# Delta-rule layer: one call inverts the triangles of several groups of a head, 27 calls in place of 48

## The chip, the core and the metric

The kernel runs on one core of a Trainium2 chip. The metric is device time in microseconds (us) of one launch, the median of several executions. The core has a matmul engine (TensorE, PE in the profile, with its weight loads as PEld), VectorE (DVE), ScalarE (ACT), GpSimd (POOL), and SyncE (SP), whose queue issues the DMAs. Each engine works through its own instructions strictly in the order in which the program was written.

## What is computed

Two layers of an encoder, for a prompt of 2048 tokens (16 tiles of 128) and one tile of 128 sample tokens: first a gated delta rule with 8 heads, then differential attention with 8 heads. The change is in the first layer. Per head and chunk the reference solves a unit lower triangular system and then carries a state from chunk to chunk:

```python
kb = k * beta[..., None]
A = jnp.where(strict, jnp.einsum("bnhid,bnhjd->bnhij", kb, k) * decay, 0.0)
sol = lax.linalg.triangular_solve(eye + A, rhs, left_side=True, lower=True, unit_diagonal=True)
...
def step(s, xs):
    u = u_i - jnp.einsum("bhcd,bhde->bhce", w_i, s)
    o = jnp.einsum("bhcd,bhde->bhce", qg_i, s) + jnp.einsum("bhij,bhje->bhie", qk_i, u)
    s = s * gl_i[..., None, None] + jnp.einsum("bhcd,bhce->bhde", kd_i, u)
    return s, o
```

The kernel takes chunks of 128 tokens, so that each tile of each head needs the inverse of one 128x128 unit triangular matrix.

## The kernel before

The tokens are taken in two halves: 9 tiles (tiles 0, 1, the sample tile, 2 to 7) and 8 tiles (8 to 15). Each half is cut into three groups: 3, 3, 3 tiles and 3, 3, 2 tiles. For each half `gdn_heads` runs the delta-rule layer, `out_proj` its output projection, then `diff_heads` and `out_proj` the attention layer. So the delta-rule stage comes twice.

No scheduler orders the work at run time. Generators (`projections`, `scans`, `others`, `inverse` and so on) write the program, and the class `Weave` (line 88) decides at build time whose next step is written, by its own estimates of when operands and buffers are ready and by a priority (`spawn`, line 221). The order so made is fixed; where its estimates are off, an engine waits.

What one head and group does in `gdn_heads` (line 955):

- `projections` (line 1023, priority 0): the projections to k, q and v, 72 matmuls of 128x384 per k, q or v in pieces of 3 (tiles `hT`, `wq`); then convolution and norms on ACT, DVE and POOL.
- `inverse` (line 1384): products of k with itself, times a decay matrix E, give X (a tile `X`, one 128x128 triangle per tile of tokens). X goes to a DRAM scratch area (`xd`), from which `blocks` (line 1335) fetches the 16x16 blocks of the diagonals, 8 per tile, one block per partition: 24 partitions for 3 tiles, 16 for 2 (tile `Lx`). DVE inverts them all at once, elementwise, in some 21 short instructions on `Lw`, `Lr`, `Lt`. The result goes through DRAM again (`wd`, tile `W`). From there PE doubles the blocks to 32, 64 and 128 by seven bursts of small matmuls, with copies on ACT or DVE between the bursts: `V,X` and `W,Y` (32x32, on four quadrants of the array), `V,X` and `W,Y` (32x32, on two), transposes of `Wf` (64x64), `F,X` (32x64) and `Wf,F` (64x64). The result is `Wf`.
- `scans` (line 1481): the state `S` goes from tile to tile. On PE this is `S,k`, then `y` on DVE, `y,Wf` on PE, `r` on ACT, `r,kd` on PE, and the new `S` on DVE, from which the next tile's `S,k` starts; `S,q` and `r,E` give the output.
- `others` (line 1007, priority -1): the gate projection of all tiles (`wz,hT`, and one quarter in `wq,hT`), which waits for nothing but its weights, and `first_outs` (line 823, priority -2), the first part of the output projection. These fill PE between the steps above.

`scans` waits for ("inv", h, gi) of one group before it takes the group's tiles. Buffers: `X` 3, `Wf` 3, `E` 4 or 5, `k` 5 or 6 (line 957), two each of `W16`, `W`, `V`, `Y`, `F`, two areas in DRAM, one `Lx` and `Lw`. 8 heads, 3 groups and 2 halves make 48 calls of `blocks`.

Of the kernel before, what the change touches and what calls it, by code (L numbers as in the profile page):

```python
# [12 lines left out]
F32 = mybir.dt.float32  # L13
# [3 lines left out]
ALU = mybir.AluOpType  # L17
# [4 lines left out]
P = 128  # L22
# [308 lines left out]
def body(ctx, tc, I, O):  # L331
# [100 lines left out]
    vs_d = [dram.tile([P, P], F32, name=f"vsd{h}") for h in range(H)]  # L432
    areas = [[dram.tile([3, n], F32, name=f"{k}{i}") for k, n in (("xd", P * P + P), ("wd", P * 16))] for i in range(2)]
    st_d = [dram.tile([P, P], F32, name=f"std{h}") for h in range(H)]
# [13 lines left out]
    def C(name):  # L448
        return loaded[name]
# [505 lines left out]
    def gdn_heads(hi_, tiles_of, pool, ahead):  # L955
        last = hi_ == len(HALVES) - 1
        NX, NWF, NE, NV, NK, NN, ND, NU = ((3, 3, 4, 2, 5, 3, 4, 3), (3, 3, 5, 2, 6, 6, 5, 4))[hi_]
        W.phase()
# [6 lines left out]
        def new(shape, tag, bufs, eng):  # L965
            return W.tile(pool, shape, F32, tag, bufs, eng)
# [368 lines left out]
        def blocks(area, nl):  # L1335

            X, Wl = (pool.tile([24, 16, 16], F32, name=k, bufs=1) for k in ("Lx", "Lw"))
            wf = Wl.rearrange("p i j -> p (i j)")
# [5 lines left out]
            yield "v"  # L1344
            T, R = (pool.tile([24, k], F32, name=nm, bufs=1) for k, nm in ((512, "Lt"), (64, "Lr")))

# [37 lines left out]
        def inverse(h, gi, d):  # L1384

            nt = len(tiles_of[gi])
            h0, h1 = slice(0, 64), slice(64, P)
            X = yield from new([P, 3, P], "X", NX, "v")
            yield ("E", h, gi),
            for i in range(nt):  # L1390
                yield from product(d, i, d["k"], X)
            W.done(("xq", h, gi))
            area = yield from W.hold(areas, "area", "sy")
            sy.dma_start(area[0][0:nt, 0:P * P].rearrange("t (p c) -> p t c", c=P), X[:, 0:nt])
            yield from blocks(area, 8 * nt)
            W16 = yield from new([P, 3, 16], "W16", 2, "sy")
            sy.dma_start(W16[:, 0:nt], area[1][0:nt].rearrange("t (p c) -> p t c", c=16))
            W.free(area)
            Wt = yield from new([P, 3, 32], "W", 2, "v")
            v.tensor_tensor(out=Wt[:, 0:nt].rearrange("p t (a c) -> p t a c", c=16),  # L1400
# [3 lines left out]
            W.free(W16)  # L1404
            V = yield from new([P, 3, 32], "V", 2, "v")
            Y = yield from new([P, 3, 32], "Y", 2, "s")
            F = yield from new([P, 3, 64], "F", 2, "s")
            pi = yield from bank("v")

            def area_of(o, n):  # L1410
                return pi[:, o:o + nt * n].rearrange("p (t c) -> p t c", c=n)

            pa, pb, pf, pt = area_of(0, 32), area_of(96, 32), area_of(192, 64), area_of(0, 64)
            quarters = [slice(32 * b, 32 * b + 32) for b in range(4)]

            def each(out, a, b):

                for o, x, y in zip(out, a, b):
                    pe.matmul(o, x, y, start=True, stop=True)

            def parts(t, rows, cols=slice(0, 32)):
                cols = cols if isinstance(cols, list) else [cols] * len(rows)
                return [t[r, i, c] for r, c in zip(rows, cols) for i in range(nt)]


            yield "v"
            v.transpose(V.rearrange("p t c -> p (t c)")[:, 0:32 * nt], Wt.rearrange("p t c -> p (t c)")[:, 0:32 * nt])
            yield "pe"
            each(parts(pa, quarters), parts(X, quarters, quarters), parts(V, quarters))
            yield "s"  # L1430
# [8 lines left out]
            yield "pe"  # L1439
            each(parts(pa, lower), parts(X, upper, lower), parts(V, upper))  # L1440
            Wf = d["Wf"] = yield from new([P, 3, P], "Wf", NWF, "g")
            e = W.either(nt * P)
            yield e
            getattr(W, e).tensor_tensor(
                out=Wf[:, 0:nt].rearrange("p t (a c) -> p t a c", c=32),
                in0=Wt[:, 0:nt, None, :].broadcast_to([P, nt, 4, 32]),
                in1=C("quart").rearrange("p (a c) -> p a c", c=32)[:, None].broadcast_to([P, nt, 4, 32]), op=ALU.mult)
            yield "s"
# [4 lines left out]
            yield "s"  # L1453
            for r, c in zip(upper, lower):
                s.copy(Wf[r, 0:nt, c], pb[r])

            for i in range(nt):
                yield "pe"
                pe.transpose(pf[h0, i], Wf[h0, i, h0], ident[0:64, 0:64])
            yield "s"  # L1460
            s.copy(F[h0, 0:nt], pf[h0])
            yield "pe"
            for c in range(64, P, 32):
                each(parts(pt, [slice(c, c + 32)], slice(0, 64)), parts(X, [h0], slice(c, c + 32)), parts(F, [h0], h0))
            W.free(X)
            yield "s"
            s.copy(F[h1, 0:nt], pt[h1])
            yield "pe"
            each(parts(pf, [h0], h0), parts(F, [h1], h0), parts(Wf, [h1], h1))
            yield "s"  # L1470
            s.copy(Wf[h0, 0:nt, h1], pf[h0])
            W.free(Wt, V, Y, F, pi)
            W.done(("inv", h, gi))

# [718 lines left out]
```

## Time and profile before

| what | value |
|---|---|
| median of 3 runs | 3585.93 us (3585.64 to 3587.45) |
| the profiled execution: its own time | 3588.79 us |
| its span (first to last instruction) | 3587.0 us |
| PE, DVE, ACT, POOL busy | 95%, 71%, 49%, 45% of the span |
| chain that ended last | PE 75%, DVE 11%, DMA 4%, POOL 4%, ACT 3% |
| first delta-rule stage | about 128 to 850 us of the span |
| second delta-rule stage | about 1870 to 2470 us |

A group's busy time is the union of its instructions. An idle time stands with the engine that ended it. One float32 matmul is two records of the trace; the listings of the program's order count it once, so 12 matmuls there are 24 in the trace.

### The profile page before, as it was taken

How to read it: one execution, taken by the hardware profiler on the slowest of the kernel's cores; microseconds unless marked ns; L12 is line 12 of the kernel's file. 1: busy time of each engine (PE TensorE's matmuls, PEld its weight loads, DVE VectorE, ACT ScalarE, POOL GpSimd, SP SyncE). 2: the span in 40 equal slices, each digit the busy share in tenths (PEclk: the TensorE clock that was granted, in tenths of full speed). 3: DMA queues.
4: the chain of work that ended last, by engine and by line, in shares of the span. 5: the costliest groups of instructions: out<-in, count | busy, mean ns of one | idle time of the engine just before them, and what ended most of it. 6: DMA issues, size and time to landing. Idle time of an engine off the chain costs nothing.

```text
span 3587.0 us, 79525 instructions
## 1 busy us (share of the span) xinstructions
PE 3420.1 (95%) x29336; PEld 3178.8 (89%) x29336; DVE 2556.4 (71%) x6345; ACT 1773.7 (49%) x5379; POOL 1622.3 (45%) x2758
## 2 busy tenths in 40 slices
PE   5999999999999999999999999998899999999988
PEld 2887789889999999998989899888899999999988
DVE  4677788775576666666467877775588888888872
ACT  3454455553354444444445555553365555555541
POOL 4344444443444434443344654444455455554442
PEclk6999999999999999999999999999999999999999
DMA  5225422235343333344531222225311112111113
GB/s 190 59 72 158 122 76 73 58 99 189 127 125 108 112 112 115 111 119 120 180 93 47 59 58 75 61 72 162 124 42 55 29 56 57 50 52 34 51 59 124
DMA packets 479420, 330.61 MB, mean 92 GB/s; under 512 B 65799, under 2 KB 442143, under 8 KB 479030
## 3 DMA queue, kind: packets, MB, share of 16 engines
q1 hardware_dynamic: 474358, 316.76, 30.0%
q0 software_dynamic: 4672, 8.78, 1.0%
q8 instruction: 230, 3.77, 0.4%
q14 instruction: 160, 1.31, 0.1%
HBM read 233.65 MB, written 91.77 MB: 91 GB/s over the span
## 4 chain that ended last, share of the span: by engine, by line
PE 75%; DVE 11%; DMA 4%; POOL 4%; ACT 3%; issue 3%; SPq 0%; POOLq 0%; DVEq 0%; ACTq 0%
PE ps L105 75%; DVE negm L105 1%; DVE Lt L105 1%; DVE p L105 1%; POOL p L105 1%; POOL fo L105 1%; DVE wq L105 1%; POOL sm L105 1%; DVE Lr L105 1%; ACT L105 1%; ACT jkg L105 1%; SPq L105 0%; DVE Lw L105 0%; DVE at L105 0%; DVE r L105 0%
## 5 line engine op out<-in xcount | busy, mean ns | idle before, releaser
L105 PE MATMUL ps<-wq,hT 128*128 128x256 f32 x6120 | 853.3, 287 | 4.4 <-DVE r L105 3.4
L105 PEld LDWEIGHTS ps<-wq,hT 128*128 128x128 f32 x6120 | 775.3, 190 | 17.5 <-DVE r L105 4.5
L105 PE MATMUL ps<-hT,wq 128*128 128x384 f32 (+1 forms) x3456 | 697.5, 341 | 2.1 <-ACT ub L105 1.6
L105 PE MATMUL ps<-wz,hT 128*128 128x256 f32 x4488 | 648.8, 291 | 14.2 <-DVE r L105 13.4
L105 PEld LDWEIGHTS ps<-wz,hT 128*128 128x128 f32 x4488 | 581.3, 193 | 23.8 <-DVE r L105 14.8
L105 PEld LDWEIGHTS ps<-hT,wq 128*128 128x128 f32 x3456 | 558.1, 190 | 15.3 <-issue 2.9
L105 ACT ACTIVATE p<-ps,negm 128x512 f32<-128x512 f32 (+3 forms) x640 | 396.9, 624 | 240.5 <-DVE negm L105 235.5
L105 DVE TENSOR_REDUCE negm<-ps 128x1 f32<-128x512 f32 (+3 forms) x640 | 377.7, 606 | 48.3 <-PE ps L105 37.9
L105 POOL TENSOR_SCALAR p<-p,fj 128x512 f32<-128x512 f32 (+2 forms) x320 | 247.1, 782 | 231.8 <-DVE fj L105 179.2
L105 PE MATMUL ps<-kst,qst 128*128 128x512 f32 (+3 forms) x1280 | 347.1, 380 | 0.4 <-ACT p L105 0.4
L105 PE MATMUL ps<-vpc,at 128*128 128x128 f32 x2176 | 294.4, 277 | 4.6 <-DVE at L105 4.0
L105 DVE SCALAR_TENSOR_TENSOR p<-p,fj,p 128x512 f32<-128x512 f32 (+2 forms) x320 | 274.2, 882 | 27.9 <-POOL p L105 27.0
L105 PEld LDWEIGHTS ps<-vpc,at 128*128 128x128 f32 x2176 | 271.4, 192 | 15.2 <-DVE at L105 8.8
L105 PEld LDWEIGHTS ps<-kst,qst 128*128 128x128 f32 x1280 | 206.6, 190 | 18.2 <-ACT p L105 2.7
L105 PE MATMUL ps<-cst_ident,p 128*128 128x128 f32 x1224 | 194.0, 275 | 16.1 <-DVE p L105 12.1
L105 POOL TENSOR_TENSOR wq<-st,wq 128x512 fp32r<-128x512 f32 x103 | 142.6, 1386 | 144.6 <-ACT wq L105 72.4
L105 ACT COPY at<-ps 128x512 f32<-128x512 f32 (+1 forms) x208 | 106.4, 512 | 188.5 <-PE ps L105 187.2
L105 ACT ACTIVATE jk<-ps 128x128 f32<-128x128 f32 (+1 forms) x212 | 80.3, 379 | 229.6 <-PE ps L105 177.2
L105 POOL TENSOR_TENSOR fo<-fo,cpow 128x1 f32<-128x1 f32 x280 | 173.9, 621 | 23.3
L105 PEld LDWEIGHTS ps<-cst_ident,p 128*128 128x128 f32 x1224 | 144.0, 141 | 25.3 <-DVE p L105 15.1
L105 POOL TENSOR_TENSOR r<-r,r 128x256 f32<-128x256 f32 (+1 forms) x144 | 106.2, 758 | 108.5 <-DVE r L105 106.7
L105 POOL TENSOR_SCALAR fo<-so,sm 128x1 f32<-128x1 f32 x136 | 51.0, 375 | 211.2 <-ACT jkg L105 210.9
(334 smaller groups left out, 6519.2 us busy)
## 6 DMA issues: line engine op xcount, KB each, us to landing
st<-in_w_in_gdn_dram SPq DMA_DIRECT2D x128, 256.0 KB
st<-in_w_in_diff_dram SPq DMA_DIRECT2D x256, 128.0 KB
x<-x SPq DMA_DIRECT2D x34, 512.0 KB
wz<-in_w_ada_dram SPq DMA_DIRECT2D x16, 1024.0 KB
sp<-in_cache_k_dram SPq DMA_DIRECT2D x64, 256.0 KB
sp<-in_cache_v_dram SPq DMA_DIRECT2D x64, 256.0 KB
zg<-zt SPq DMA_DIRECT2D x68, 128.0 KB
og<-o SPq DMA_DIRECT2D x136, 64.0 KB
```

Source lines behind the costliest of these rows:

```text
L105: r = f(*args, **kw)
```

## The change

`inverse` keeps the products that make X, one group at a time, and signals ("X", h, gi). A new generator `invert` takes a batch of groups, waits for all their X, and does the rest for all tiles of the batch together. `batches_of` sets the batches: in the first half the first group alone and the other two together (1 and 2 groups, 3 and 6 tiles), in the second half the whole head (8 tiles); the last head of each half stays group by group. That makes 7 x 2 + 3 calls in the first half and 7 + 3 in the second, 27 in all. `blocks` then works on up to 48 or 64 partitions. The scratch areas, `Lx`, `Lw`, `Lt`, `Lr` and the tiles of a call grow to 6 or 8 tiles; `W16`, `W` and `F` exist once instead of twice, V and Y become the two halves of F, and X has 4 buffers instead of 3. All matmuls stay: a burst of small matmuls has those of all tiles of its batch. `Wf` stays one tile per group, 3 in all, taken for the whole batch before its last bursts.

```diff
-        NX, NWF, NE, NV, NK, NN, ND, NU = ((3, 3, 4, 2, 5, 3, 4, 3), (3, 3, 5, 2, 6, 6, 5, 4))[hi_]
+        NX, NWF, NE, NV, NK, NN, ND, NU = ((4, 3, 4, 2, 5, 3, 4, 3), (4, 3, 5, 2, 6, 6, 5, 4))[hi_]
+        NTI = (6, 8)[hi_]
...
-            X, Wl = (pool.tile([24, 16, 16], F32, name=k, bufs=1) for k in ("Lx", "Lw"))
+            X, Wl = (pool.tile([8 * NTI, 16, 16], F32, name=k, bufs=1) for k in ("Lx", "Lw"))
...
         def inverse(h, gi, d):
 
-            nt = len(tiles_of[gi])
-            h0, h1 = slice(0, 64), slice(64, P)
-            X = yield from new([P, 3, P], "X", NX, "v")
+            batch = next(b for b in batches_of(h) if gi in b)
+            if gi == batch[0]:
+                W.spawn(invert(h, batch), 3)
+            X = d["X"] = yield from new([P, 3, P], "X", NX, "v")
             yield ("E", h, gi),
-            for i in range(nt):
+            for i in range(len(tiles_of[gi])):
                 yield from product(d, i, d["k"], X)
             W.done(("xq", h, gi))
+            W.done(("X", h, gi))
+
+        def batches_of(h):
+
+            if h == H - 1:
+                return [[gi] for gi in range(NGr)]
+            return [[0], list(range(1, NGr))] if hi_ == 0 else [list(range(NGr))]
+
+        def invert(h, batch):
...
+            at = [(gi, i) for gi in batch for i in range(len(tiles_of[gi]))]
+            nt = len(at)
+            yield ("X", h, batch[0]), "sy"
             area = yield from W.hold(areas, "area", "sy")
-            sy.dma_start(area[0][0:nt, 0:P * P].rearrange("t (p c) -> p t c", c=P), X[:, 0:nt])
+            for gi in batch:
+                yield ("X", h, gi), "sy"
+                sy.dma_start(...)
             yield from blocks(area, 8 * nt)
-            W16 = yield from new([P, 3, 16], "W16", 2, "sy")
+            W16 = yield from new([P, NTI, 16], "W16", 1, "sy")
...
-            Wt = yield from new([P, 3, 32], "W", 2, "v")
+            Wt = yield from new([P, NTI, 32], "W", 1, "v")
...
-            V = yield from new([P, 3, 32], "V", 2, "v")
-            Y = yield from new([P, 3, 32], "Y", 2, "s")
-            F = yield from new([P, 3, 64], "F", 2, "s")
+            F = yield from new([P, NTI, 64], "F", 1, "v")
...
-            Wf = d["Wf"] = yield from new([P, 3, P], "Wf", NWF, "g")
+            for gi in batch:
+                U[h, gi]["Wf"] = yield from new([P, 3, P], "Wf", NWF, "g")
...
-            W.done(("inv", h, gi))
+            for gi in batch:
+                W.done(("inv", h, gi))
```

The order moves everywhere in the two stages. Three places on PE matter below. First, one burst of small matmuls in the second stage: `V_30380,X_29967` before, where a group of two tiles has its own call:

```order
L105 MATMUL ps_81<-V_30380,X_29967 32x32 x8
L105 MATMUL ps_76<-hT_23573,wq 128x256 x6
L105 MATMUL ps_78<-r,kd_29567 128x128
L105 MATMUL ps_81<-W_30369,Y_30385 32x32 x8
L105 MATMUL ps_77<-k_29726 128x128
L105 MATMUL ps_76<-hT_23573,wq 128x256 x9
```

And in the changed kernel, where `F_30396` holds V and Y, and the three X are those of one head:

```order
L105 MATMUL ps_80<-F_30396,X_30070 32x32 x2
L105 MATMUL ps_82<-q_29909,k_29887 128x128
L105 MATMUL ps_80<-W_30386,F_30396 32x32 x32
L105 MATMUL ps_79<-cst_ident,k_30077 128x128 x3
L105 MATMUL ps_77<-cst_ident,q_30175 128x128 x3
L105 MATMUL ps_78<-wq,hT_22508 128x256 x9
```

The bursts of three groups have become one; counted over the whole program there are 337 bursts of small matmuls before and 189 after, and 1450 runs of the large projection matmuls before and 1392 after.

Second, the end of the second delta-rule stage on PE before. `wq,hT` is the gate projection, its last 21 matmuls stand first; `S,k`, `y,Wf` and `r,kd` are the state's steps; after 22 rows of such steps the output projection (`wz,hT_31711`) comes in:

```order
L105 MATMUL ps_77<-wq,hT_23573 128x256 x21
L105 MATMUL ps_80<-k_31317 128x128
...
L105 MATMUL ps_82<-y,Wf_31897 128x128
L105 MATMUL ps_81<-V_32168,X_31812 32x32 x12
L105 MATMUL ps_82<-r,kd_31089 128x128
...
L105 MATMUL ps_81<-V_32168,X_31812 32x32 x6
L105 MATMUL ps_75<-wz_30618,hT_31711 128x256 x3
L105 MATMUL ps_81<-W_32157,Y_32169 32x32 x6
```

The same place in the changed kernel, from its last gate projection to its first output projection:

```order
L105 MATMUL ps_81<-wq,hT_23259 128x256 x3
L105 MATMUL ps_80<-r,kd_29343 128x128
L105 MATMUL ps_78<-S,q_28953 128x128
L105 MATMUL ps_78<-r,E_29135 128x128
L105 MATMUL ps_77<-S,k_29129 128x128
L105 MATMUL ps_77<-y,Wf_30577 128x128
...
L105 MATMUL ps_81<-r,E_30342 128x128
L105 MATMUL ps_78<-S,k_30077 128x128
L105 MATMUL ps_76<-wz_29857,hT_30746 128x256 x9
```

There are 81 rows between them now, 32 of them `S,k`, `y,Wf` or `r,kd` (6 before), and no large matmul.

Third, a place in the middle of the second stage in the changed kernel, behind the last matmuls of one quarter of the gate projection (`wz_25955`); `hT_22508,wq` is the next projection to k:

```order
L105 MATMUL ps_82<-wz_25955,hT_23259 128x256 x3
L105 MATMUL ps_78<-r,kd_26293 128x128
...
L105 MATMUL ps_78<-S,k_26160 128x128
L105 MATMUL ps_78<-y,Wf_27655 128x128
L105 MATMUL ps_75<-hT_22508,wq 128x384 x6
```

17 rows with 9 steps of the state stand there without a large matmul. Two more such places have 7 steps (first stage, near its last head) and 5 steps (second stage). Before, the only other place with more than three steps has 4.

## Rows read from the trace of the kernel before

**Rows 1.** Busy time by stretches: stretch, its length, PE, PEld, DVE, ACT, POOL, granted clock, DMA.
```profile
128.00:850.00 722.00, 697.07 (x6335) 622.15 (x6334) 552.53 (x1538) 368.05 (x1205) 321.65 (x704) 0.98 0.35 96
1870.00:2470.00 600.00, 570.49 (x5422) 524.07 (x5421) 463.04 (x1258) 327.98 (x1083) 295.27 (x597) 0.97 0.25 68
```

**Rows 2.** What PE waited for, 1860 to 2500 us: total us, times, longest.
```profile
PE ps L105 <- DVE S L105: 9.4, 4, 5.3
PE ps L105 <- DVE y L105: 6.4, 7, 2.8
PE ps L105 <- DVE V L105: 4.8, 3, 4.1
```

**Rows 3.** Instructions that touch tile Lx: count, durations, first and last start, forms.
```profile
L105 DVE COPY Lw<-Lx x48: 155/167/726, 138.1 to 2422.6; 24x12 f32<-24x12 f32 x40, 16x12 f32<-16x12 f32 x8
```

**Rows 4.** Timeline of DVE: start us, us, instruction; first of one block inversion, and its follower.
```profile
2409.24 0.17 DVE L105 COPY Lw<-Lx 24x12 f32<-24x12 f32 x1
...
2415.26 0.33 DVE L105 SCALAR_TENSOR_TENSOR S<-S,g_eGl,ps 128x128 f32<-128x128 f32 x1
```

**Rows 5.** Timeline of PE: each burst of small matmuls with the row behind it.
```profile
159.83 0.64 PE L105 MATMUL ps<-V,X 32*32 32x32 f32 x24 [0.51 <-DVE V L105]
160.40 0.49 PE L105 MATMUL ps<-q,k 128*128 128x128 f32 x2
...
2397.62 0.46 PE L105 MATMUL ps<-V,X 32*32 32x32 f32 x12
2398.01 0.49 PE L105 MATMUL ps<-k 128*128 128x128 f32 x2
...
2404.12 0.66 PE L105 MATMUL ps<-F,X 64*32 64x64 f32 x12
2404.71 0.49 PE L105 MATMUL ps<-q,k 128*128 128x128 f32 x2
...
2441.18 0.35 PE L105 MATMUL ps<-V,X 32*32 32x32 f32 x16
2441.45 0.63 PE L105 MATMUL ps<-wz,hT 128*128 128x256 f32 x3
...
2450.39 0.42 PE L105 MATMUL ps<-F,X 64*32 64x64 f32 x8
2450.74 0.44 PE L105 MATMUL ps<-cst_ident,k 128*128 128x128 f32 x2
```

**Rows 6.** Timeline of PE: a short and a long run of large matmuls, with the rows behind.
```profile
2394.72 0.62 PE L105 MATMUL ps<-wq,hT 128*128 128x256 f32 x3
2395.18 0.38 PE L105 MATMUL ps<-k 128*128 128x128 f32 x2
...
2410.61 2.72 PE L105 MATMUL ps<-wq,hT 128*128 128x256 f32 x21
2413.17 0.38 PE L105 MATMUL ps<-k 128*128 128x128 f32 x2
2413.39 0.39 PE L105 MATMUL ps<-S,q 128*128 128x128 f32 x2
```

**Rows 7.** Timeline of PE at the end of the second stage, idle time before in brackets.
```profile
2415.74 0.46 PE L105 MATMUL ps<-S,k 128*128 128x128 f32 x2 [1.74 <-DVE S L105]
...
2418.74 0.42 PE L105 MATMUL ps<-S,k 128*128 128x128 f32 x2
...
2432.72 0.79 PE L105 MATMUL ps<-S,q 128*128 128x128 f32 x2 [5.35 <-DVE S L105]
...
2434.46 1.01 PE L105 MATMUL ps<-wz,hT 128*128 128x256 f32 x3
```

**Rows 8.** Busy time by stretches at both stages' ends, columns as in rows 1.
```profile
840.00:845.00 5.00, 2.73 (x21) 2.05 (x20) 3.13 (x8) 2.32 (x9) 2.05 (x4) 1.00 0.89 269
845.00:852.00 7.00, 7.00 (x48) 7.00 (x48) 2.99 (x7) 1.33 (x3) 2.25 (x4) 0.76 0.78 229
...
2422.00:2440.00 18.00, 10.45 (x83) 8.26 (x84) 13.07 (x29) 4.81 (x16) 7.75 (x10) 0.53 0.44 131
```

## What I expect, before the result

> **What bounds the kernel now.** I read the busy time by stretches first, for the two delta-rule stages alone. In the first stage PE is busy for 697.07 of 722 us and DVE for 552.53, in the second 570.49 of 600 and 463.04 [rows 1]. So PE is the bound of both stages, and what PE loses outside its matmuls is 24.9 + 29.5 = 54.4 us. No change of DVE work alone can give more than that. The second view is what PE waited for: in the second stage DVE S 9.4 us, DVE y 6.4 us, DVE V 4.8 us [rows 2]. S and y are the state's steps, V the first transposed block inverse. The third view is PE's timeline, for what the small matmuls cost while PE is busy [rows 5], and what its large runs lose when they are cut [rows 6]. The last is the end of the second stage, where PE ran out of large matmuls before the state was done [rows 7], and its granted clock there [rows 8].
>
> **The change part by part.** All matmuls stay and the block inversions fall from 48 [rows 3] to 27. One block inversion holds DVE for 2415.26 - 2409.24 = 6.0 us [rows 4]. More partitions at equal columns should not lengthen it much: the forms of 16 and 24 partitions stand in one group there [rows 3], and no row shows 48 or 64. So DVE loses some 21 x 6.0 = 126 us of work. DVE is no bound, so of this only waits of PE behind a block count. The idle times that PE spent on S and y are 15.8 us in the second stage [rows 2]; one of 1.74 us ends just when the block of 2409.24 us is over [rows 4, 7]. The last head keeps its own blocks, and with it the longest wait, 5.35 us [rows 7]. I take 4 us off, bounds 0 and 9.
>
> *Bursts of small matmuls.* A call has seven bursts, so 21 calls fewer are 147 bursts fewer; the program's order says the same, 337 against 189. A burst of 24 records of 32x32 takes 160.40 - 159.83 = 0.57 us to the next row, one of 12 takes 0.39 [rows 5]. If a burst is a fixed part and a part per record, this is 0.015 us a record and 0.21 us fixed. F,X with 12 records takes 0.59 and with 8 takes 0.35 [rows 5], a line with no fixed part at all, and the other bursts lie between by shape. I take 0.15 us a burst: 147 x 0.15 = 22 us off PE. The bound to the good is 147 x 0.21 = 31 us. The bound to the bad comes from groups of two and three tiles. 16 records of V,X take 0.27 us, 24 take 0.57 [rows 5], 0.30 us for one tile more. If that went on, 8 tiles in one burst would take 0.57 + 5 x 0.30 = 2.07 us where three bursts took 0.57 + 0.57 + 0.27 = 1.41, and 6 tiles 1.47 against 1.14. With two such bursts a call, and F,X at 0.06 us a record (0.26 and 0.13 us more), that is 1.6 us lost in each of 7 calls and 0.8 us in 7 others, 17 us. I stay near the good end, because 24 and 12 records differ in quadrants alone, and the changed bursts add tiles on the same four quadrants in the same way.
>
> *Runs of large matmuls.* Three of 128x256 take 0.46 us, 21 take 2.56, or 0.122 each [rows 6]. A cut thus costs 0.46 - 0.366 = 0.09 us. The order has 1392 such runs where it had 1450: 58 x 0.09 = 5 us off.
>
> *What is later.* A head's state in the second stage starts only when all its groups are inverted, so that the state's steps move back against the projections and the gate work, which fill PE between them. At the stage's end the order leaves 81 rows without a large matmul, 32 of them steps; before, 22 rows and 6 steps. What that is worth: before, from 2413.17 to 2434.46 it took 21.3 us [rows 6, 7]. Its PE work is about 13 single matmuls at 0.22 us (2413.17 to 2413.39 [rows 6]) and 2.6 us of bursts and transposes, 5.5 us, so 15.8 us were lost, much of it behind the last block. After, three steps take 3.0 us where nothing is in the way (2415.74 to 2418.74 [rows 7]), so 32 steps take 32 us, and the one block that stands in this chain takes 6.0 more. At a granted clock of 0.53, nearly the level of 1.2 GHz, that this stretch already shows from 2422 to 2440 us [rows 8], an S,q takes 0.79 us and not 0.46 [rows 7]; with up to 0.3 us on each step the length is 38 to 48 us, and I take 42. The work in it is about 57 x 0.22 + 18 bursts at 0.35 + 1.5 us = 20 us. The loss is 22 us against 15.8: 6 us more, bounds 0 and 14.
>
> *Three other bare places* with 9, 5 and 7 steps, at 1.0 us a step and less 3.7, 2.0 and 4.6 us of their own matmuls: 5 + 3 + 2 = 10 us more, bounds 4 and 15. The clock fell at a bare place before as well: behind 840 to 845 us, where PE was busy for 2.73 of 5, the next 7 us ran at 0.76 [rows 8]. I add 5 us for that, bounds 0 and 8. These places wait for free k tiles and for the next gate weights, which no faster engine brings.
>
> *The first stage's end* gets better: gate work stands there up to the output projection. Before, 840 to 845 us had 2.3 us of idle PE and 845 to 852 us lost about 24% of 7 us [rows 8]; with the idle times just before I take 6 us off, bounds 0 and 6.
>
> *DMA, ACT and POOL* cost nothing here. A call's transfers get larger and there are fewer; the wait for them lies in the inverse, ahead of which the order puts projections. If that cover is missing, it is the second rival.
>
> **The sum**: -4 - 22 - 5 + 6 + 10 + 5 - 6 = -16 us, against the profiled execution's own 3588.79 us: 3572.8. The median before lies 2.9 us below that, so I expect 3570 us, faster by 0.45%. All bounds together would be -47 and +54.
>
> **The rivals.** *A, a matmul's price is its own.* If a small matmul costs the same in any burst, the term of 22 us is gone, and the time is 3570 + 22 = 3592, no change. For it: F,X has no fixed part, and 16 records of V,X took 0.27 us [rows 5]. Against it: 24 and 12 records do not stand as two to one. The Trainium skill's page "TensorEngine Tiling (Array Packing)", section Performance Considerations, has a rule that would give this rival: each matmul carries an overhead of about 60 cycles, whatever its columns. By that page 60 cycles at 2.4 GHz are an estimated 25 ns, 0.60 us for 24 records and 0.30 for 12; the rows have 0.57 and 0.39, so the trace agrees with it for the long burst and not for the short one.
>
> *B, slower: the inverse of a batch is waited for.* Only one set of W16, W and F is left, and a whole head waits for the last group's X, the round through DRAM and seven bursts. Where the order thinks the inverse done too early, PE stands still with everything behind it, projections too. The trace has this once: PE waited 4.1 us for V at the start of the second stage [rows 2]. If each of the 14 batched calls waits 4.1 us, that is 57 us; with half of them 29 us, and the time is 3570 + 29 = 3599. It decides the sign from (16 + 7) / 14 = 1.6 us a call, 7 us being 0.2% of the time.
>
> *C, more is won*: the waits of PE on S, y and V, 20.6 us in the second stage [rows 2], nearly vanish, as DVE has an eighth less to do (126 of 1015.6 us [rows 1]). Then some 20 us more go: 3550.
>
> That the change does not do what it says is no rival: the order shows the bursts joined.
>
> **How the numbers follow.** Forecast 0.52, A 0.18, B 0.17, C 0.13. A measurement of this kernel tells 0.2%, 7 us, from no change, so faster ends at 3578.8 and slower begins at 3593.1. The forecast and C lie under the first but for a tenth: 0.58 faster. A, and what is left of the forecast: 0.24 same. B and A's upper end: 0.18 slower. The range takes in C's time and most of B: 3547 to 3598.
>
> **What would show it.** In the trace after: V,X (now F,X) bursts of 64 records near 1.2 us, not 2.07 and not 1.41; PE idle in the middle of both stages not above today's; 35 to 48 us between the last gate matmul and the first output projection of the second stage; 27 COPY Lw. It is wrong if PE waits for F or Wf in the batched heads (B), or if the bursts scale with their matmuls (A).

## The result and the profile after

The changed kernel takes 3615.28 us (median; 3609.9 to 3618.16) against 3586.69 us for the kernel before in the same series. The ratio is 1.0076, 95% interval 1.0058 to 1.0093: **slower by 0.8%**, where 3570 us and a gain were forecast. The profiled execution took 3616.82 us, its span is 3615.0 us.

The loss lies in one place. I mark stages by the first matmul of the second part of an output projection (`wx,hT`; its first part, `wz,hT`, fills PE earlier). The first delta-rule stage ends by this mark at 866.1 us before and 866.5 after. From the mark in the first half's last output projection (1718.9 us before, 1717.3 after) to the mark of the second delta-rule stage (2482.2 and 2513.85) it is 763.3 us before and 796.55 after, 33 us more; I call this stretch the second stage. What lies between the two stages is 2.0 us shorter, all that follows them 3.6 us. Busy time by stretches, columns as in [rows 1]: the second stage of before,

```profile
1718.90:2482.20 763.30, 728.99 (x6679) 675.17 (x6678) 552.23 (x1438) 399.87 (x1263) 366.70 (x712) 0.98 0.29 84
```

and of after, with the first stage under it:

```profile
1717.30:2513.85 796.55, 750.46 (x6684) 710.12 (x6682) 486.22 (x1185) 376.18 (x1171) 315.47 (x661) 0.94 0.30 82
128.00:850.00 722.00, 692.75 (x6339) 626.47 (x6338) 514.03 (x1397) 354.24 (x1170) 323.30 (x689) 0.98 0.35 100
```

DVE has 66 us less to do in the second stage, as meant. PE does the same matmuls (a few records are missing in each trace), but is idle for 46.1 us and not 34.3, and busy for 21.5 us more, at a mean granted clock of 0.94 and not 0.98. To see which matmuls take that time I add, for every matmul, the time from its start to the next one's start, less idle time:

| second stage, us | before | after |
|---|---|---|
| idle | 34.3 | 46.1 |
| large projection matmuls (3360) | 511.7 | 514.6 |
| bursts of small matmuls (1984 records) | 70.2 | 80.0 |
| single matmuls of 128x128 and the like | 147.1 | 155.9 |

In the first stage the bursts take 79.3 us before and 80.9 after. So in neither stage have the joined bursts saved anything in sum. What PE waited for, 1870 to 2520 us of after, answers [rows 2]:

```profile
PE ps L105 <- DVE y L105: 19.4, 18, 4.3
PE ps L105 <- DVE F L105: 7.1, 4, 3.4
PE ps L105 <- ACT r L105: 2.9, 9, 0.6
PE ps L105 <- DVE k L105: 2.6, 2, 1.6
PE ps L105 <- DMA S<-std: 1.9, 1, 1.9
PE ps L105 <- DVE v L105: 1.7, 1, 1.7
PE ps L105 <- DVE S L105: 1.6, 2, 0.9
```

The waits for S have gone from 9.4 us to 1.6, those for y from 6.4 to 19.4. One of them on PE,

```profile
1949.88 9.16 PE L105 MATMUL ps<-hT,wq 128*128 128x384 f32 x63
1961.53 0.49 PE L105 MATMUL ps<-y,Wf 128*128 128x128 f32 x2 [2.49 <-DVE y L105]
```

and what DVE did meanwhile (idle time before in brackets):

```profile
1951.64 0.35 DVE L105 SCALAR_TENSOR_TENSOR E<-E,g_nG,cst_lev 128x128 f32<-128x128 f32 x1 [2.27 <-DMA E<-grow]
...
1955.03 0.17 DVE L105 COPY Lw<-Lx 64x12 f32<-64x12 f32 x1 [2.51 <-DMA Lx<-xd]
...
1960.54 0.68 DVE L105 TENSOR_REDUCE Lw<-Lt 64x64 f32<-64x512 f32 x1
1961.14 0.33 DVE L105 SCALAR_TENSOR_TENSOR y<-ps,g_neG,nv 128x128 f32<-128x128 f32 x1
```

DVE stands twice for data, then inverts a block for 6.1 us (64 partitions, and 24 took 6.0 [rows 4]), and y, for which PE waits, stands behind all of it. PE has 63 matmuls to cover that and runs out. The same place comes in four heads. Over the stage DVE's waits for the two transfers are, after,

```profile
DVE Lw L105 <- DMA Lx<-xd: 20.8, 10, 2.6
DVE E L105 <- DMA E<-grow: 20.7, 14, 2.5
```

where before it waited 8.6 us for Lx and not at all for E. The last head of the first stage has such a place too, on PE:

```profile
741.33 0.80 PE L105 MATMUL ps<-nv,Wf 128*128 128x128 f32 x2 [8.94 <-DVE S L105]
...
753.47 0.77 PE L105 MATMUL ps<-wz,hT 128*128 128x256 f32 x2
```

DVE had waited there 4.03 us for Lx, and S stood behind the block; PE had no large matmul from 729.19 to 753.47 us.

Last, the end of the second stage, which answers [rows 7]:

```profile
2414.26 0.60 PE L105 MATMUL ps<-wq,hT 128*128 128x256 f32 x3
2414.86 0.49 PE L105 MATMUL ps<-r,kd 128*128 128x128 f32 x2
...
2446.74 0.80 PE L105 MATMUL ps<-S,k 128*128 128x128 f32 x2 [1.93 <-DMA S<-std]
2451.85 0.79 PE L105 MATMUL ps<-y,Wf 128*128 128x128 f32 x2 [4.31 <-DVE y L105]
...
2462.28 0.80 PE L105 MATMUL ps<-y,Wf 128*128 128x128 f32 x2
...
2467.01 0.80 PE L105 MATMUL ps<-y,Wf 128*128 128x128 f32 x2 [0.44 <-DVE y L105]
...
2473.39 1.32 PE L105 MATMUL ps<-wz,hT 128*128 128x256 f32 x9
```

58.5 us pass between the last gate matmul and the output projection; it was 21.3. One tile's step takes 4.7 us (2462.28 to 2467.01). The clock there, in the columns of [rows 8]:

```profile
2420.00:2470.00 50.00, 38.27 (x272) 30.20 (x271) 22.63 (x71) 16.58 (x66) 11.49 (x29) 0.50 0.24 68
```

### The profile page after: what moved, and what is told of

Same layout as the page of the kernel before. It is cut to its first block, busy times and chain, and to the rows that moved or that the text cites. A ratio compares the mean times of both kernels' runs of the same rounds, so it can differ in the third digit from the quotient of the medians.

```text
span 3615.0 us, 78745 instructions
## 1 busy us (share of the span) xinstructions
PE 3440.9 (95%) x29336; PEld 3220.9 (89%) x29336; DVE 2439.9 (67%) x5936; ACT 1732.7 (48%) x5248; POOL 1568.7 (43%) x2690
## 4 chain that ended last, share of the span: by engine, by line
PE 73%; DVE 10%; DMA 6%; POOL 4%; issue 3%; ACT 3%; SPq 0%; POOLq 0%; DVEq 0%; ACTq 0%
PE ps L105 73%; DVE negm L105 2%; DVE p L105 1%; DMA E<-grow 1%; POOL fo L105 1%; POOL p L105 1%; DMA Lx<-xd 1%; DVE wq L105 1%; DVE Lt L105 1%; DMA xd<-X 1%; DVE r L105 1%; POOL sm L105 1%; DMA st<-in_w_in_diff_dram 1%; DVE at L105 1%; SPq L105 0%
## 5 line engine op out<-in xcount | busy, mean ns | idle before, releaser
L105 PEld LDWEIGHTS ps<-wq,hT 128*128 128x128 f32 x6120 | 778.3, 191 | 21.5 <-DVE r L105 4.5
L105 PEld LDWEIGHTS ps<-hT,wq 128*128 128x128 f32 x3456 | 566.1, 192 | 10.6 <-issue 4.1
L105 DVE SCALAR_TENSOR_TENSOR p<-p,fj,p 128x512 f32<-128x512 f32 (+2 forms) x320 | 274.4, 883 | 28.6 <-POOL p L105 27.8
L105 POOL TENSOR_TENSOR wq<-st,wq 128x512 fp32r<-128x512 f32 x87 | 119.6, 1376 | 186.6 <-ACT wq L105 104.8
```

Source lines behind the costliest of these rows:

```text
L105: r = f(*args, **kw)
```

## The experiments

All times are compared with the kernel before on the same chip, whose median lay between 3585.7 and 3592.8 us. "Calls" are block inversions (48 before, 27 after). The second stage and PE's idle time in it are those of the profiled execution, measured as above; the column before them is the first stage's end. These columns stand on one execution each: e1 and after have the same order in the first stage and differ there by 7 us, after and e7 (below) have it up to the bare end of the second stage and differ there by 15.

| run | calls | us | ratio, 95% interval | first stage's end | second stage | PE idle |
|---|---|---|---|---|---|---|
| before | 48 | 3586.69 | 1 | 866.1 | 763.3 | 34.3 |
| after | 27 | 3615.28 | 1.0076 (1.0058 to 1.0093) | 866.5 | 796.6 | 46.1 |
| e1 first stage only | 41 | 3582.14 | 0.9979 (0.9968 to 0.9990) | 873.6 | 762.0 | 29.6 |
| e3 by group | 48 | 3616.10 | 1.0075 (1.0059 to 1.0091) | 895.8 | 762.7 | 27.9 |
| e4 first group apart | 34 | 3569.91 | 0.9948 (0.9931 to 0.9966) | 865.9 | 750.1 | 25.3 |
| e5 last two by group | 29 | 3605.85 | 1.0046 (1.0029 to 1.0063) | 867.5 | 793.3 | 52.3 |
| e10 two sets | 34 | 3567.72 | 0.9943 (0.9926 to 0.9959) | 867.6 | 750.4 | 30.8 |
| e16 last group apart | 34 | 3571.79 | 0.9943 (0.9928 to 0.9958) | 868.4 | 748.3 | 26.6 |
| e18 first stage two, then one | 34 | 3615.78 | 1.0062 (1.0044 to 1.0080) | 911.0 | 752.3 | 28.5 |
| e20 whole, then apart | 30 | 3575.98 | 0.9961 (0.9946 to 0.9976) | 867.1 | 757.5 | 32.9 |
| e17 last head too | 32 | 3560.48 | 0.9915 (0.9900 to 0.9931) | 864.3 | 749.6 | 25.7 |
| e8 short blocks, after | 27 | 3574.97 | 0.9964 (0.9948 to 0.9980) | 864.7 | 759.6 | 27.8 |
| e19 short blocks, before | 48 | 3552.02 | 0.9888 (0.9870 to 0.9906) | 848.3 | 745.3 | 21.4 |

**Which part costs it: e1, e3, e4, e5.** The edits are all in `batches_of`:

```diff
             if h == H - 1:                        # e1: if h == H - 1 or hi_ == 1:    e5: if h >= H - 1 - hi_:
                 return [[gi] for gi in range(NGr)]     # e3: this line alone
-            return [[0], list(range(1, NGr))] if hi_ == 0 else [list(range(NGr))]
+            return [[0], list(range(1, NGr))]     # e4
```

e1: 

> Groups are joined in the first delta-rule stage alone, in the second each group has its own call (NX 4 and the single W16, W and F stay). Theory T, the second stage's whole-head calls cost the 28 us: the state waits for them, steps stand bare at the stage's end and the clock falls there: 3583 to 3592 us, no difference from before that counts. Rival L, long bursts of small matmuls cost PE more than short ones: half of the calls that lost stay joined, 3598 to 3606. Rival S, one set of W16, W and F in place of two makes every call wait for the one before: 3608 or more, since single sets stay and there are more calls.

e3: 

> No groups are joined at all; what stays of the change is NX 4, one set of W16, W and F, V and Y inside F, and the inverse as a stream of its own. T: 3584 to 3597 us (its order leaves 33 rows with 11 steps at the second stage's end, where before had 22 with 6, so a few us are lost there). L: 3584 to 3590, as before. S: 3608 or more.

e4: 

> In the second stage a head's first group has a call of its own and the other two are joined, as in the first stage, 34 calls in place of 27. The head's state can start with the first group, and the order leaves 21 rows with 7 steps bare at the stage's end, not 81 with 32. T: 3582 to 3595 us. L: bursts of 40 records in place of 64, so half of the loss stays, 3598 to 3606. S: 3610 or more.

e5: 

> In the second stage the last two heads, not only the last, have a call for each group. The middle of the stage is as in the changed kernel; the bare end shrinks from 81 rows with 32 steps to 43 with 17, while 10 steps stand bare a little earlier. T: about half of the end's loss comes back, 3596 to 3606 us. L: one whole-head call fewer out of seven, 3611 to 3615. S: 3611 to 3618.

e1 gives the loss back, 33 us: the whole heads of the second stage cost it, which is the place that theory T names; its reason is not tested by this run. e4 says more. With seven calls more than the changed kernel it is 45 us faster, and faster than before by 0.5%: joining pays as long as a head isn't one piece. L and S fall with it for this stage, as they had 3598 us or more. PE's waits, 1870 to 2465 us, show the difference; y, 19.4 us in the changed kernel, is down to

```profile
PE ps L105 <- DVE y L105: 1.1, 2, 0.7
```

and DVE's wait for `E<-grow` from 20.7 us to 0.2. A bare place with 7 steps, 16.8 us long, stands ahead of the stage's end, where no stretch without a large matmul is longer than 4.6 us:

```profile
2344.00 0.39 PE L105 MATMUL ps<-r,kd 128*128 128x128 f32 x2
...
2360.80 1.41 PE L105 MATMUL ps<-wz,hT 128*128 128x256 f32 x5
```

e5 met its figure, 9 us back, though not by the end alone: the end fell from 58.5 to 29.3 us, and a place of 21.1 us opened before it, at 2319 us, so that the profiled second stage is only 3 us shorter. e3 missed T by 19 us and hit S's number, but in the other stage: its second stage is as short as before's, and the 30 us are in the first, which ends at 895.8. There the changed kernel wins back by joining what its own form costs by group. Why that form costs 30 us there is open: single sets (S) are a candidate that no run tests in the first stage.

**Are the single sets to blame, and does it matter which group stands apart: e10, e16, e18.** e10 is e4 with `W16`, `W`, `F` twice in the second stage and `X` 3 times; e16 has `[[0, 1], [2]]` there, e18 has it in the first stage and e4's cut in the second:

```diff
-            return [[0], list(range(1, NGr))]
+            return [[0], [1, 2]] if hi_ == 0 else [[0, 1], [2]]     # e16
+            return [[0, 1], [2]] if hi_ == 0 else [[0], [1, 2]]     # e18
```

e10: 

> The first group apart and the other two joined in the second stage, as before, now with two sets of W16, W and F there (and NX 3 to make room). If the single sets still cost time where groups are joined: 3555 to 3564 us. If they don't, 3566 to 3580, with what another order does (33 rows with 10 steps stand bare at the stage's end, where it was 21 with 7).

e16: 

> In the second stage a head's first two groups are joined and the third has a call of its own, [0, 1] and [2], where the run of 3570 us had [0] and [1, 2]: the same number of calls and of block inversions, but the state can start only when six of eight tiles are inverted, not three. If the start of the state sets the time (the theory): between the two, 3578 to 3600. If the number of calls does: 3566 to 3576.

e18: 

> The kernel of 3570 us with the first stage's groups joined the other way round, [0, 1] and [2] in place of [0] and [1, 2]; the second stage keeps [0] and [1, 2]. If the start of the state sets the first stage too: 5 to 20 us slower, 3575 to 3590. If the first stage has filling work for PE whatever the state does: 3565 to 3574.

A second set is worth nothing in the second stage where groups are joined (3567.72 against 3569.91). e16 contradicts my theory in its plain form: with the state able to start only after six tiles it is as fast as with three. So it isn't the start of the state as such. What e4 and e16 share, and the changed kernel lacks, is a cut in the head, with room for state work of the same head between two calls; that this room is the cause is argued, not shown by itself. e18 loses 46 us, all in the first stage, which ends at 911.0. With e3 this shows that the first stage is sensitive to how calls are cut; by what, the runs don't settle.

**Does the lag add up: e20.**

```diff
-            return [[0], list(range(1, NGr))] if hi_ == 0 else [list(range(NGr))]
+            return [list(range(NGr))] if hi_ == 1 and h < 4 else [[0], list(range(1, NGr))]
```

> Second stage: heads 0 to 3 as whole heads, heads 4 to 6 with the first group apart, the last by group. If the late start of the state adds up from head to head and is paid at the stage's end: the end stays long, 25 to 45 us without a large matmul, though its last heads are apart, and the time is 3588 to 3602. If only the heads near the end count: as the run of 3570 us, 3566 to 3578, with no long end.

Half of each. The end is 27.4 us long (2404.84 to 2432.25) though its last heads are cut. That whole heads early delay the state up to the end is not shown by this: before and e1, with no whole head in this stage, have bare ends of 21.3 and 22.5 us. The time, 3576, is only 6 us above e4's. So the loss is no price per whole head: four of the seven cost 6 of the 45 us, though in them PE still waits for y, 2.36 us at 1960.08 and 1.72 at 2117.83. In this profile the clock stays full behind both; in the changed kernel's it fell behind such waits (last section).

**Is it the wait in front of the block, or the block: e12, e11, e14, e13, e15, e8, e19.** The later landing is three lines behind the load of `Lx`, in the changed kernel (e12), e4 (e11), e17 (e14) and before (e13):

```diff
+            for k in W.parts_of(X):
+                W.ready[k] = W.ready[k][0] + 1500, None
+            W.cur["at"], W.cur["by"] = W.ready[k]
```

e12: 

> The changed kernel with whole heads, but where the order is made, the block's data (Lx) are taken to land 1.5 us later, so that DVE gets other work before each block. No instruction is added. Theory W, DVE stands still for Lx in front of a block and y or S stands behind it: DVE's waits for Lx (20.8 us in ten calls of the second stage) fall below 10, PE's waits for y in the middle of the stage go, and since the order still leaves 83 rows with 33 steps bare at the stage's end, that stays at 55 to 60 us: 3588 to 3603. Rival V, the block's own 6.1 us in front of y are enough: y is waited for as before, 3608 to 3620.

e13: 

> The kernel before with the same later landing, nothing joined: a control. DVE waited for Lx for only 8.6 us there, so little is to be won, and the order leaves 48 rows with 16 steps bare at the second stage's end in place of 22 with 6, which costs 10 to 15 us: 3588 to 3605. If the later landing is good by itself, whatever the calls: 3565 to 3580.

e11: 

> The first group apart and the other two joined in the second stage (as in the run of 3570 us), and the later landing: the order leaves no more than 9 rows with 4 steps bare in either stage, and that at the second stage's end. W: 3545 to 3560. V: 3564 to 3576, as without it.

e14: 

> As the run before it, with the last head's groups joined in the same way, 32 calls. The order leaves one place of 6 rows with 4 steps bare in both stages. W: 3542 to 3560, and the wait of 9 us behind the block in the last head of the first stage goes. V: 3562 to 3576.

Measured: e12 3607.65 (1.0054, 1.0039 to 1.0069), e13 3648.82 (1.0164, 1.0148 to 1.0181), e11 3582.34 (0.9986, 0.9976 to 0.9995), e14 3580.76 us (0.9978, 0.9968 to 0.9989). This failed as a means. DVE's waits for Lx did not shrink in e12:

```profile
DVE Lw L105 <- DMA Lx<-xd: 21.9, 8, 5.9
```

They became fewer and longer, and each of the four has a first stage that ends 9 to 39 us later than without it (e13 904.8, e11 884.5, e12 880.8, e14 873.7). It also shows what bare rows in the order are worth: e11's order has at most 9 in one place, e4's 21, and e11's second stage is 1 us shorter (748.9 against 750.1); what e11 loses against e4 is in the first stage (884.5 against 865.9).

e15 is meant to take the wait away with no other order, on all engines: in the second stage, from its second head on, a block reads the other area, which was written one call before.

```diff
-            sy.dma_start(X[0:nl], window(area[0]))
+            W.tc.keep_in_program_order(sy.real.dma_start(X[0:nl], window(areas[area is areas[0]][0])))
+            W.account("sy", "dma_start", (X[0:nl], window(area[0])), {})
```

> The changed kernel in the same order on each engine, but in the second stage a block inversion reads the blocks that the call before left in the other DRAM area (it inverts older data), so that nothing lands late: DVE needn't stand for Lx (20.8 us in ten calls), the block keeps its 6.1 us. If DVE's stand for the data holds y and S back: PE's waits for y (19.4 us) fall below 10 and the time to 3588 to 3602. If the block's own length is what holds them: the waits for y stay above 14 and the time is 3607 to 3618.

3612.08 us (1.0060, 1.0042 to 1.0078), as the changed kernel. The test came out weak, since it took only a part of the wait; DVE's and PE's waits are

```profile
DVE Lw L105 <- DMA Lx<-xd: 14.9, 7, 3.3
```

```profile
PE ps L105 <- DVE y L105: 13.7, 15, 4.1
```

and behind `E<-grow`, which stands ahead of it, DVE still waits 21.0 us. PE's wait for y lies between my two marks of 10 and 14. What it shows is that 6 us less of standing for Lx brought no more than 3 us. No run takes the wait for `E<-grow` away alone.

e8 and e19 keep the order and every DMA and leave out the last step of each block, `m = 8`:

```diff
-                        v.tensor_tensor(**kw)
+                        if m == 4: v.tensor_tensor(**kw)
+                        else: W.account("v", "tensor_tensor", (), kw)     # and the same for tensor_reduce
```

e8: 

> The changed kernel without the last step of each block inversion (the two 512-element products and their sums, 3.4 of 6.1 us on DVE; the corner of 8x8 is left out). All else is in the same order. Theory Y, y behind a block holds PE for 2 us in each head and the clock falls behind it: the waits for y, 19.4 us, go and with them the low clock, 3588 to 3600. Rival E, only the bare end counts: two blocks stand in it, so 7 us go and little else, 3604 to 3610.

e19: 

> The kernel before without the last step of each block inversion (48 calls, 3.4 us of DVE each; the corner of 8x8 is left out), all else in the same order: the control for the short blocks in the changed kernel, which took 40 us off. If DVE's blocks hold PE back there too (so that DVE was no spare engine before either): 3530 to 3565. If they do so only where groups are joined: 3575 to 3588.

Here are the largest effects of all. In e8 a block takes 2.3 us and not 6.1 (1946.36 to 1948.70), and the kernel is 40 us faster, more than either theory allowed. The wait for y, 1860 to 2500 us, halves, while DVE stands for `E<-grow` as long as before, 20.4 us:

```profile
PE ps L105 <- DVE y L105: 9.3, 14, 2.5
```

The end stays at 55.3 us (2377.42 to 2432.70); the middle, from 1713.0 to 2377.42, is 664.4 us where after has 697.6 (1717.3 to 2414.86). Of these 33 us 13 are idle time of PE (28.7 to 15.2) and 20 its busy time, at a mean clock of 0.99 and not 0.96. How much of the 20 belongs to the blocks is open, as the clock differs between executions: e7's profile (below) has the same order with whole blocks and takes 682.2 us there, with an idle time of 27.4 and a clock of 0.98.

e19, the control, moves as well. DVE's busy time over the whole span fell by 167 us (2556.4 to 2389.2), and the kernel by 35, 0.21 for each, half of it in either stage (866.1 to 848.3, 763.3 to 745.3). In the changed kernel it fell by 85 us (2439.9 to 2354.6) and brought 40, 0.47 for each, of which the profiles put 2 into the first stage (866.5 to 864.7) and 37 into the second (796.6 to 759.6). So the blocks held PE back in part before, and in the changed kernel a microsecond of them cost about twice as much.

**What a small matmul costs: e6.**

```diff
-                for o, x, y in zip(out, a, b):
-                    pe.matmul(o, x, y, start=True, stop=True)
+                for _ in range(2):
+                    for o, x, y in zip(out, a, b):
+                        r = (pe.real if _ else pe).matmul(o, x, y, start=True, stop=True)
```

> The changed kernel, each burst of small matmuls (F,X, W,F and Wf,F) issued twice in a row, all else in the same order: it measures what a small matmul costs in a long burst. Theory R, each record has its price (the trace after: 48 records 1.33 us, 64 records 1.84, so 32 ns for each 32x32 record, 54 and 58 for the larger ones): 3264 x 0.032 + 544 x 0.054 + 272 x 0.058 = 150 us more, 3740 to 3775. Rival P, the prediction's price (a fixed part for each burst, 0.015 us a record): 3264 x 0.015 us and some 30 to 45 for the larger ones = 80 to 95 us more, 3690 to 3712.

3744.32 us (1.0432, 1.0388 to 1.0477), 129 us more than the changed kernel: within R's range, far from P's. Where the clock is full a burst of 96 records takes 2.45 us (184.40 to 186.85) and one of 128 takes 3.46 (2050.97 to 2054.43), so the added 48 and 64 cost 23 and 25 ns each. The bursts of after themselves, with the row behind each:

```profile
181.49 1.40 PE L105 MATMUL ps<-F,X 32*32 32x32 f32 x48
182.82 0.49 PE L105 MATMUL ps<-k 128*128 128x128 f32 x2
...
1891.57 1.91 PE L105 MATMUL ps<-F,X 32*32 32x32 f32 x64
1893.40 0.62 PE L105 MATMUL ps<-hT,wq 128*128 128x256 f32 x3
...
1898.55 1.09 PE L105 MATMUL ps<-F,X 32*32 32x32 f32 x32
1899.57 0.49 PE L105 MATMUL ps<-q,k 128*128 128x128 f32 x2
```

64 records on four quadrants take 1.83 us, where three bursts took 0.57 + 0.57 + 0.27 = 1.41 [rows 5]; 48 take 1.33 where two took 1.14; 32 on two quadrants take 1.02, where three took 0.39 + 0.39 + 0.25 = 1.03 (0.25 is the usual burst of 8 before). In one burst on two quadrants the price is 0.032 us a record at any length, without a fixed part.

But the number of records does not set the price alone. 24 records on two quadrants take 0.77 us as one burst of after, 12 in a row on each quadrant (first two lines), and 0.58 in e6, where a burst of 12 comes twice and 6 stand in a row (its 24 records fill several rows, of which the first is shown, and the row behind them):

```profile
187.86 0.84 PE L105 MATMUL ps<-F,X 32*32 32x32 f32 x24
188.63 0.49 PE L105 MATMUL ps<-q,k 128*128 128x128 f32 x2
```

```profile
158.36 0.40 PE L105 MATMUL ps<-F,X 32*32 32x32 f32 x10
...
158.94 0.63 PE L105 MATMUL ps<-wz,hT 128*128 128x256 f32 x3
```

A burst of 24 on four quadrants, doubled, goes from 0.57 to 0.93 us, so its added records cost 15 ns each (151.72 to 152.65), where those behind 12 and 16 in a row cost 23 and 25. The starts of the single records in the trace show where it comes from: in the burst of 181.49 us they are 32 ns apart, but around the 12th, the 24th and the 36th, where by the kernel's order the quadrant changes, seven steps take 0.12 us together and not 0.22. The kernel writes a burst quadrant by quadrant, all tiles in each (`parts`), so in a joined call more records stand in a row on each quadrant, and the passes between quadrants become fewer. A burst written tile by tile was not tried.

**Is the end long because of the clock: e7.**

```diff
             pe.matmul(pc[:, P:2 * P], Wf, y, start=True, stop=True)
+            extra(h, gi, pc[:, 3 * P:4 * P], c, d)     # two matmuls of 128x128; the same behind r,kd and r,E
```

> The changed kernel with 60 matmuls of 128x128 more, two behind y,Wf, two behind r,kd and two behind r,E of the last ten steps of the second stage, where steps stand bare (their results are not used). All else is in the same order. Theory C, the bare end is long because PE is idle there and its clock falls to half: the end of 58.8 us shrinks to 45 to 52, and the time to 3602 to 3609. Rival D, the end is as long as the chain of PE, DVE and ACT makes it, whatever the clock: 58 to 72 us there (13 us if all 60 lie on the path), 3615 to 3628.

3611.19 us (1.0064, 1.0044 to 1.0083), no difference from after that counts. The profiled execution, 3595.79 us, was the fastest, so only its end is read here:

```profile
2398.44 0.49 PE L105 MATMUL ps<-r,kd 128*128 128x128 f32 x2
...
2454.38 1.32 PE L105 MATMUL ps<-wz,hT 128*128 128x256 f32 x9
```

```profile
2400.00:2450.00 50.00, 39.33 (x398) 33.55 (x399) 24.37 (x78) 18.67 (x73) 12.43 (x31) 0.90 0.26 74
```

The end takes 55.9 us at a clock of 0.90 with 60 matmuls more (some 13 us of work), and took 58.5 at 0.50 without them. So, in these two executions, the low clock cost about what the added matmuls cost; neither theory's number was met, and how long the end would be at full clock without them stays open.

**The best version: e17**, e4 with the two lines on `h == H - 1` taken out.

> The kernel of 3570 us (first group apart, two joined) with the last head's groups joined in the same way in both stages, 32 calls in place of 34. The order differs at the ends of both stages alone. If fewer calls pay there: 3560 to 3568. If the last head's state waits for its joined call: 3570 to 3580.

3560.48 us, 0.85% faster than before and 1.5% faster than the changed kernel; the second stage's columns as in [rows 1]:

```profile
1714.10:2463.70 749.60, 723.94 (x6688) 684.92 (x6687) 506.25 (x1300) 386.09 (x1214) 349.68 (x681) 0.98 0.32 90
```

## Why the prediction was wrong, step by step

Two steps failed outright. The term for the bursts, -22 us, measured +11 us (1.6 in the first stage, 9.8 in the second), because records in a row on one quadrant cost 0.032 us each where I had 0.015. And in the term for what is later the bare end was put at 42 us and took 58.5, with a loss some 22 us above before's where I had 6. Beside them the path was wrong: the step y of the state stands behind the block of a whole head on DVE, and PE waits 19.4 us for it, which stands in no term. The figures below overlap, as the low clock is in several of them; they don't add up to the 33 us.

- **DVE is no bound, -4 us (0 to -9).** Wrong. I took PE's direct waits for S and y as all that DVE's blocks could cost. e19 shortened the blocks alone and won 35 us. At its 0.21 us for each us of DVE, 21 calls of 6.0 us would be worth an estimated 26 us, had the calls that stay cost no more than before. Of e19's 18 us in the second stage 13 are idle time (34.3 to 21.4) and 5 are busy time, at a mean clock of 0.99 and not 0.98. The ceiling that I drew from PE's idle time, 54.4 us, held.
- **Bursts, -22 us (+17 to -31).** The largest error of size. In the first stage the bursts got 1.6 us longer, in the second 9.8. At full clock a whole-head call pays 0.5 us more for its bursts (0.42 on each of the two long ones and 0.18 for F,X, less 0.28 for Wf,F and 0.23 for the transposes), 3.5 us in seven calls. The rest is the low clock: 389 of the 1984 records ran at a granted clock below 0.95 and took 21.0 us, where before 88 did, in 4.1; in e6 a burst of 128 took 5.65 us where the clock was 0.50 and 3.46 where it was full. My split into a fixed part of 0.21 us and 0.015 us a record was right for the rows that I used, 24 and 12 records with 6 in a row on each quadrant. It failed at "in the same way": more tiles put more records in a row on each quadrant, and there a record costs 0.032. My bad bound was the better estimate, and so was rival A's time, which lets the bursts save nothing. The page of the Trainium skill that I set against it, "TensorEngine Tiling (Array Packing)", Performance Considerations, gives an overhead of about 60 cycles a matmul, an estimated 25 ns. e6's 23 and 25 ns for each added record of the long bursts agree with it; the 15 ns in bursts of 24 and the 32 ns in a row on one quadrant do not, and the measurement decides.
- **Cuts of large runs, -5 us.** Not seen: the large matmuls took 2.9 us less up to the end of the first stage (495.6 to 492.7, from the start of the span) and 2.9 more in the second.
- **The end of the second stage, +6 us (0 to 14), 42 us long.** The work in it was right (20.7 us by the median time of each matmul, forecast 20), the length was 58.5 us. A tile's three steps take 4.3 to 4.7 us at half clock, 1.4 to 1.6 a step where I had 1.0 and at most 1.3, and the block, the state's load (`S<-std`) and `W` come on top. The loss there is 38 us against 15 before.
- **Bare places, +10 us (4 to 15), and the clock, +5 (0 to 8).** The three places lost 18.5, 4.2 and 2.7 us, 25 in all; the first, in the last head of the first stage, holds the wait of 8.94 us for S behind the block. The clock I had put at 5 us: by stretches of 5 us, the share that it lacked adds up to 15 us in the second stage before and 51 after, the bare end among them.
- **The first stage's end, -6 us.** The stage as a whole came out equal, 866.1 and 866.5.
- **Rival B** was nearest in time (3599) and in kind, something waits for a batch, but not in place. PE waited for F 7.1 us in four places, not in each call, and not for Wf. What is late is y, a step of another head's state that needs nothing of the batch but stands behind its block on DVE. **Rival C** fell: the waits for S went, those for y came in their place.

Of the marks I had set, 27 `COPY Lw` were right:

```profile
L105 DVE COPY Lw<-Lx x27: 155/167/355, 137.2 to 2443.1; 24x12 f32<-24x12 f32 x12, 48x12 f32<-48x12 f32 x7, 64x12 f32<-64x12 f32 x7, 16x12 f32<-16x12 f32 x1
```

The 64 records at 1.83 us lie between my two bounds of 1.41 and 2.07, the end lies outside its 35 to 48 us, and PE's idle time in the middle of the stages is above before's, 29.2 us against 24.9 in the first (128 to 850 us) and 28.7 against 20.6 in the second (up to the bare end).

That e4 came out at 3570 us is luck, no merit of the sum. The gain there is not the bursts', which I had put at 22: they took 74.7 us in its second stage and 70.2 before. PE's idle time fell by 9 us (34.3 to 25.3), which with e19 points to DVE, for which I had 4 us, and the large matmuls took 7 us less (511.7 to 504.5), by what is open.

## What to carry to other kernels

Join small calls only as far as work that starts on their first results still finds a place between two calls: one cut through each head was worth 45 us in the second stage here. On which side of the middle group it was made changed 2 us there and 46 in the first stage, so try the cuts stage by stage. An engine that is 70% busy is not free for that: shorten its work in the same order and see what the kernel gives back (here 0.21 us per us before, 0.47 in the changed kernel) before you price its removal. Take the price of a small matmul from bursts in which the same thing grows as in your change: here the records in a row on one quadrant, which neither the number of records nor that of quadrants tells.

## What the chip showed unexpectedly

The clock does not follow the wait alone. A wait of PE for y at the same place of the same order was followed by a fall in one execution and not in another. After and then e7, the wait and the next stretch of 5 us (clock in the third column from the end):

```profile
2279.53 0.49 PE L105 MATMUL ps<-y,Wf 128*128 128x128 f32 x2 [1.91 <-DVE y L105]
```

```profile
2280.00:2285.00 5.00, 5.00 (x33) 5.00 (x32) 4.07 (x10) 3.93 (x9) 1.79 (x4) 0.66 0.37 79
```

```profile
2265.46 0.49 PE L105 MATMUL ps<-y,Wf 128*128 128x128 f32 x2 [1.67 <-DVE y L105]
```

```profile
2265.00:2270.00 5.00, 4.54 (x39) 4.54 (x40) 4.55 (x13) 3.65 (x9) 1.58 (x4) 1.00 0.34 70
```

Of the four such waits of about 2 us all were followed by a lower clock in the changed kernel's profile, and two in e7's. At 0.66 a stretch of 5 us lacks 1.7, so by this estimate one such wait costs 2 us in one execution and up to 3.7 in the next. Single profiles differ by more than that: e1 and after have the same order in the first stage and end it at 873.6 and 866.5 us.
